# Moving the next head's queries and keys ahead of most value strips, and starting the output projection beside the last head, in a two-layer encoder trunk

## The chip, the cores and the metric

One core of one Trainium2 chip runs the whole kernel in one launch. The metric is the device time of one launch in microseconds, the median of a few runs. The engines are named as in the profile: PE is TensorE (matrix products), with PEld its weight loads; DVE is VectorE; ACT is ScalarE; POOL is GpSimd; SP is SyncE, which here only issues DMAs. Each engine runs its own instructions in a fixed order, and waits in that order.

## What is computed

The reference is a trunk of two layers over 1024 prompt tokens and 256 sample tokens, 1024 features wide, in float32. The change lies in layer 0, attention over a neighbourhood on a token grid 64 wide, with 16 heads of 64 features and a gate:

```
proj = h @ w_in ;  q, k, v, g = split(proj, 4)
for every row r of the grid, every head:
    s = q_r . k(rows around r, columns around) ;  s = where(mask, s + bias, -1e30)
    o = softmax(s) . v
return (o * silu(g)) @ w_out          # then + residual
```

Layer 1 is a gated delta network in chunks, which the change does not touch.

## The kernel before

**How numbers are held.** [...] A block of tokens is 512, 512 or 256 wide (`BLK`). `load_w` (L1085) brings a weight in: SP loads `wraw` (one buffer), `wh` is a cast of it on POOL while `a["hi"]` is set (L1094) and on ACT otherwise (L1096), and `wl` is a negative copy on ACT (L1100) to which a DMA issued by POOL adds the weight once more (L1101). `wh` and `wl` have three buffers each.

**The loop over heads** (L333). The attention of head h is a generator, and a small scheduler, `Side`, lets it advance by a step each time that the projection beside it has issued so many columns: `side.add(chain, delay, pace)` starts it `delay` columns from now, and each step's own distance is multiplied by `pace`. Beside head h's attention the loop issues the products of head h+1's queries and keys (`qk_head`, three blocks: 24 matmuls each of 512, 512 and 256 columns), and then, by h modulo 4: the gates of the next pair of heads (`g_pair`, h%4 of 1 and 2), or a part of the next four heads' values. These are ten strips of 128 tokens, V0 to V9, each 24 matmuls of 256 columns: strips 0 to 3 at h%4 of 3, strips 4 to 9 at the next h%4 of 0, ahead of `qk_head(h + 1)` (`v_quad`, L114). ACT and DVE each make one pass over a strip (L110, L111) to move it out of PSUM.

**One head.** `qk_head` ends with two DMAs on ACT's queue which copy the keys, in their high part KH (L195) and low part KL (L196), from the upper 64 partitions to the lower; the scores of the head need both. The attention has five units j of two score tiles: scores on PE (L279 with KH, L280 with KL; L298 and L299 for the sample tokens), softmax (DVE L216, ACT L217 with the exponential, DVE L218 and L219), transposes on PE into `pt` (L236), its split in `ph` on ACT (L240) and `pl` on DVE (L241), the products with the values into O (L256), and their way out with the gate (ACT L262, DVE L263 and L264). After an odd head the pair's O is spilled to DRAM (L323).

**After the loop** the spilled outputs of the first seven pairs are loaded back (L361) and split in OH (ACT, L362) and OL (L363: POOL for even k, DVE for odd k), and the output projection `w_o` runs, i = 0 to 7 by blocks b; its first evacuations are on DVE (L381). PSUM has three banks `mm` for projections.

**What sets the order.** The program's order gives each instruction its priority, and a list scheduler then orders each engine's queue from it when the kernel is built. So instructions that the text has after the loop can stand beside the last heads: the first output products do already in the kernel before.

```
            side.add(attention(h, qkk, V, G, O), 14000 if h % 4 == 1 else 2000, (1.6, 1.2, 1.5, 1.35)[h % 4])
            if h % 4 == 0:
                v_quad(q, V, [s for s in range(10) if s not in V], side)
            if h < 15:
                qkk = qk_head(h + 1, side)
```

Of the kernel before, what the change touches and what calls it, by code (L numbers as in the profile page):

```python
# [8 lines left out]
F32 = mybir.dt.float32  # L9
F32R = mybir.dt.float32r  # L10
BF16 = mybir.dt.bfloat16
AF = mybir.ActivationFunctionType
# [5 lines left out]
KD = 8  # L18
BLK = [(0, 512), (512, 512), (1024, 256)]
# [16 lines left out]
def layer0(ctx, tc, a, h1_out):  # L36
# [136 lines left out]
    with st:  # L173
# [92 lines left out]
        def attention(h, qkk, V, G, O):  # L266
# [55 lines left out]
            if h % 2 and h < 15:  # L322
                nc.sync.dma_start(a["o_dram"][h // 2], O)  # L323

        done = {}
        side = Side()
        a["hi"] = True
# [5 lines left out]
        for h in range(16):  # L333
            done[h] = 0
            G = GS[h // 2]
            V = nV if h % 4 == 0 else V
            side.add(attention(h, qkk, V, G, O), 14000 if h % 4 == 1 else 2000, (1.6, 1.2, 1.5, 1.35)[h % 4])
            side.tick(0)
            q = (h + 1) // 4
            if h % 4 == 0:  # L340
                v_quad(q, V, [s for s in range(10) if s not in V], side)
            if h < 15:
                qkk = qk_head(h + 1, side)
            if h % 4 in (1, 2) and h < 14:
                p = h // 2 + 1
                g_pair(p, GS[p], range(3), side)
            elif h % 4 == 3 and h < 15:
                nV = {}
                v_quad(q, nV, range(4), side)
            side.drain()  # L350
            if h % 2 and h < 15:
                O = ap.tile([128, T], F32, name="O", bufs=1)
        a["hi"] = False
        wo = [load_w(tc, a, a["w_o"][i]) for i in range(2)]
        OH, OL = parts(xp)
        for b, (t0, n) in enumerate(BLK):
            for k in range(KD):
                t = O[:, t0:t0 + n]
                if k < KD - 1:
                    t = OL[k][b].bitcast(F32)  # L360
                    nc.sync.dma_start(t, a["o_dram"][k, :, t0:t0 + n])  # L361
                nc.scalar.activation(OH[k][b], t, AF.Copy)  # L362
                (nc.vector if k % 2 else nc.gpsimd).tensor_sub(OL[k][b], t, OH[k][b])  # L363

    tc.keep_in_program_order(nc.scalar.preload_act_table_set("natural_log"))
    with pool(tc, "h1", 1) as hp, pool(tc, "rms1", 2) as rp, banks(tc, "pmm1", 2) as pmm1:
# [5 lines left out]
        for i in range(8):  # L372
            if i > 1:
                wo.append(load_w(tc, a, a["w_o"][i], raw=rp if i % 2 else None, keep=rp if i == 4 else None))
            h1 = hp.tile([128, NP], F32, name=f"p{i}")
            xt = rp.tile([128, NP], F32, name="xres")
            nc.sync.dma_start(xt, x_in[i, :, :NP])
            for b, (t0, n) in enumerate(BLK[:2]):
                ps = pmm.tile([128, 512], F32, name="mm")
                proj(nc, ps, *wo[i], OH, OL, b)  # L380
                nc.vector.tensor_add(h1.rearrange("p (r c) -> p c r", c=64)[:, 32 * b:32 * b + 32],  # L381
                                     nat(ps), nat(xt[:, t0:t0 + n]))
            nc.sync.dma_start(h1_out[i, :, :NP], h1)
            for b, (t0, n) in enumerate(BLK[:2]):
                H[b][i] = h1[:, t0:t0 + n]
                square(nc, rp, H[b][i], acc[b], i == 0)
# [751 lines left out]
                self.step(c)  # L1138


def proj_steps(nc, ps, wh, wl, XH, XL, b):
    for k in range(KD):
        for i, (w, x) in enumerate(((wh, XH), (wh, XL), (wl, XH))):
            nc.tensor.matmul(ps, w[:, k, :], x[k][b], start=(k == 0 and i == 0), stop=(k == KD - 1 and i == 2))  # L1144
            yield BLK[b][1]
# [20 lines left out]
def parts(xp):  # L1166

    return [[[xp.tile([128, n], F32R, name=f"x{p}{k}_{b}") for b, (t0, n) in enumerate(BLK)] for k in range(KD)]
            for p in "hl"]
# [228 lines left out]
```

## Time and profile before

| | |
|---|---|
| median of 3 runs | 2283.3 us (2281.1 to 2285.49) |
| the profiled execution | 2280.4 us, its span 2278.6 us |
| mean granted TensorE clock | 0.975 of full speed |
| busy: PE, DVE, ACT, POOL | 95%, 68%, 48%, 25% of the span |
| layer 0's heads in the span | about 85 to 685 us |

A row of the timeline gives the start from the span's beginning and the duration; matmuls overlap, so what one costs is the distance between the starts of two of them. The bracket behind a row is idle time of the engine before it, and what ended that.

### The profile page before, as it was taken

The page shows a single profiled execution, that of the slowest core. Times are in us where ns is not written, and L with a number is a line of the kernel's source. Part 1 is how long each engine was busy: PE and PEld are TensorE (multiplying, and loading weights), DVE is VectorE, ACT ScalarE, POOL GpSimd, SP SyncE. Part 2 cuts the span into 40 slices and gives each one's busy share as a digit, 9 for nine tenths or more (in the row PEclk, how much of TensorE's full clock was granted, in tenths as well). Part 3 has the DMA queues.
Part 4 walks back from the last instruction along what each step waited for, and adds up shares of the span by engine and source line. Part 5 has one row for each costly group of instructions (what it writes and reads, how often), then busy time and mean ns, then how long its engine had stood idle before and what let it go on. Part 6 is the DMA issues. An engine that isn't in the chain of part 4 may idle for free.

```text
span 2278.6 us, 34055 instructions
## 1 busy us (share of the span) xinstructions
PE 2171.5 (95%) x12502; PEld 1889.8 (83%) x12502; DVE 1545.8 (68%) x3419; ACT 1104.2 (48%) x2282; POOL 572.9 (25%) x621
## 2 busy tenths in 40 slices
PE   8999999899989889999899999999899999999998
PEld 7889889789768768888788888888788888877887
DVE  5676576576683649597687978878457666676444
ACT  6455445445462454434335445344356666654233
POOL 2110110111020332313223322233166766610000
PEclk9999999999999889999899999999899999999999
DMA  5443442434447244444354444553566656567322
GB/s 178 110 111 79 100 106 78 109 92 104 114 134 212 73 102 123 123 126 117 92 147 143 108 143 114 141 146 91 173 207 176 173 168 184 150 213 235 112 97 84
DMA packets 146119, 301.14 MB, mean 132 GB/s; under 512 B 44688, under 2 KB 67216, under 8 KB 144928
## 3 DMA queue, kind: packets, MB, share of 16 engines
q1 hardware_dynamic: 124480, 232.89, 32.6%
q0 software_dynamic: 12384, 45.09, 11.2%
q10 hardware_dynamic: 9088, 20.98, 3.1%
q8 instruction: 99, 1.62, 0.3%
q14 instruction: 68, 0.56, 0.1%
HBM read 212.97 MB, written 75.45 MB: 127 GB/s over the span
## 4 chain that ended last, share of the span: by engine, by line
PE 69%; DVE 15%; DMA 6%; ACT 5%; issue 3%; POOL 1%; SPq 0%; DVEq 0%; ACTq 0%; POOLq 0%
PE mm L1144 41%; PE mm L1160 4%; PE k L908 3%; DVE acc L460 3%; PE o L880 2%; PE u L880 2%; PE k L899 2%; PE o L921 2%; PE O L256 2%; DVE X L581 2%; DVE tmp L579 2%; PE pt L236 2%; DMA KH<-KH 1%; DMA vT<-qkv_spill 1%; PE m L607 1%
## 5 line engine op out<-in xcount | busy, mean ns | idle before, releaser
L1144 PE MATMUL mm<-xh,wh 128*128 128x512 f32 (+1 forms) x1920 | 701.8, 366 | 11.7 <-ACT wh L1096 5.9
L1144 PE MATMUL mm<-xh,wl 128*128 128x512 f32 (+1 forms) x1920 | 699.8, 365 | 4.7 <-DVE wl L1098 2.2
L1144 PE MATMUL mm<-xl,wh 128*128 128x512 f32 (+1 forms) x1920 | 702.2, 366 | 0.0
L1144 PEld LDWEIGHTS mm<-xh,wh 128*128 128x128 f32 x1920 | 369.2, 192 | 56.9 <-ACT wh L1096 6.4
L1144 PEld LDWEIGHTS mm<-xh,wl 128*128 128x128 f32 x1920 | 368.6, 192 | 47.5 <-DVE wl L1098 2.4
L1144 PEld LDWEIGHTS mm<-xl,wh 128*128 128x128 f32 x1920 | 369.1, 192 | 43.0 <-issue 0.2
L460 DVE SCALAR_TENSOR_TENSOR acc<-raw,cw,acc 128x1282 f32<-128x1282 f32 x128 | 203.1, 1587 | 43.1 <-ACT acc L458 41.5
L1096 ACT ACTIVATE wh<-wraw 128x1024 fp32r<-128x1024 f32 x94 | 98.9, 1055 | 110.9 <-PE mm L1144 88.0
L1094 POOL CAST wh<-wraw 128x1024 fp32r<-128x1024 f32 x30 | 31.5, 1049 | 473.6 <-PE mm L1144 339.7
L1144 PE MATMUL mm<-yh,wh 128*128 128x512 f32 (+1 forms) x384 | 137.5, 359 | 2.3 <-ACT yh L1018 1.9
L1144 PE MATMUL mm<-yh,wl 128*128 128x512 f32 (+1 forms) x384 | 137.0, 358 | 1.2 <-DVE wl L1098 1.2
L1144 PE MATMUL mm<-yl,wh 128*128 128x512 f32 (+1 forms) x384 | 137.7, 360 | 0.3 <-DVE yl L1019 0.3
L912 DVE TENSOR_TENSOR vl<-k,vh 128x256 fp32r<-128x256 f32 x160 | 67.1, 424 | 69.3 <-ACT vh L911 64.8
L463 ACT ACTIVATE th<-acc 128x1282 f32<-128x1282 f32 x32 | 40.9, 1277 | 149.4 <-DVE acc L460 149.4
L241 DVE TENSOR_TENSOR pl<-pt,ph 128x512 fp32r<-128x512 f32 (+2 forms) x144 | 75.4, 540 | 55.1 <-ACT ph L240 54.0
L240 ACT ACTIVATE ph<-pt 128x512 fp32r<-128x512 f32 (+2 forms) x144 | 67.3, 478 | 76.1 <-PE pt L236 69.1
L1100 ACT ACTIVATE wl<-wraw 128x1024 fp32r<-128x1024 f32 x86 | 90.8, 1055 | 22.4 <-PE mm L1144 9.4
L217 ACT ACTIVATE P<-P,mx 128x384 f32<-128x384 f32 (+1 forms) x128 | 74.9, 585 | 51.0 <-DVE mx L216 50.1
L455 ACT ACTIVATE raw<-mm 128x512 f32<-128x512 f32 (+1 forms) x96 | 49.4, 520 | 97.4 <-PE mm L1144 96.9
L1160 PE MATMUL mm<-wh,xl 128*128 128x256 f32 x320 | 92.3, 289 | 0.3 <-POOL xl L65 0.3
L1160 PE MATMUL mm<-wl,xh 128*128 128x256 f32 x320 | 92.1, 288 | 0.4 <-DVE wl L1098 0.4
L1160 PE MATMUL mm<-wh,xh 128*128 128x256 f32 x320 | 92.2, 289 | 0.0
(316 smaller groups left out, 4885.6 us busy)
## 6 DMA issues: line engine op xcount, KB each, us to landing
wraw<-w_qkv SPq DMA_DIRECT2D x32, 512.0 KB, 3.9
wl<-w_qkv POOLq DMA_DIRECT2D x32, 512.0 KB, 7.3
qkv_spill<-th SPq DMA_DIRECT2D x32, 512.0 KB, 2.7
wraw<-w_go SPq DMA_DIRECT2D x32, 512.0 KB, 3.6
Al<-e_spill SPq DMA_DIRECT2D x8, 1280.0 KB, 7.3
qe<-eg_spill SPq DMA_DIRECT2D x16, 640.0 KB, 8.1
wraw<-w_qk SPq DMA_DIRECT2D x16, 512.0 KB, 3.8
wl<-w_qk POOLq DMA_DIRECT2D x16, 512.0 KB, 9.0
```

Source lines behind the costliest of these rows:

```text
L217: nc.scalar.activation(Pv, Pv, AF.Exp, scale=-1.0, bias=mx[:, 0:1], accum_out=mx[:, 1:2])
L240: nc.scalar.activation(view(ph), view(pt), AF.Copy)
L241: nc.vector.tensor_sub(view(pl), view(pt), view(ph))
L455: nc.scalar.activation(r[:, t0 + o:t0 + o + n], ps[:, :n], AF.Copy)
L460: nc.vector.scalar_tensor_tensor(acc, r[:, i:i + m], cw[:, f, i:i + 1], acc, op0=OP.mult, op1=OP.add)
L880: self.tc.nc.tensor.matmul(ps, w[x], v[y], start=(first and i == 0), stop=(i == 2))
L908: nc.tensor.matmul(pw, W[:, d, cs[d]], Y[d], start=True, stop=True)
L912: nc.vector.tensor_sub(vl, pw, vh)
L1096: nc.scalar.activation(wh, raw, AF.Copy)
L1100: nc.scalar.activation(wl, raw, AF.Copy, scale=-1.0)
L1144: nc.tensor.matmul(ps, w[:, k, :], x[k][b], start=(k == 0 and i == 0), stop=(k == KD - 1 and i == 2))
L1160: nc.tensor.matmul(ps, x[k][b][:, cc], w[:, k % 4, :], start=(k == 0 and i == 0), stop=(k == KD - 1 and i == 2))
```

## The change

It does three things. At h%4 of 0 only strips 4 and 5 come before `qk_head(h + 1)`, and strips 6 to 9 behind it. The attention of the heads with h%4 of 1 starts 2000 columns after it is added instead of 14000, at pace 1.5 instead of 1.2, and heads 14 and 15 run at pace 0.75. And in the step of head 15 the first two `w_o` slices are loaded, the spilled outputs of blocks 0 and 1 are split (k = 0 to 6, the subtractions all on POOL), and three output products, (i, b) = (0,0), (1,0) and (0,1), are begun with k = 0 to 6, each holding one of the three `mm` banks; k = 7, which is head 14's and 15's own output, follows after the loop.

```diff
+        def o_parts(b, ks):
+            t0, n = BLK[b]
+            for k in ks:
+                t = O[:, t0:t0 + n]
+                if k < KD - 1:
+                    t = OL[k][b].bitcast(F32)
+                    nc.sync.dma_start(t, a["o_dram"][k, :, t0:t0 + n])
+                nc.scalar.activation(OH[k][b], t, AF.Copy)
+                (nc.vector if k % 2 and (b == 2 or k == KD - 1) else nc.gpsimd).tensor_sub(OL[k][b], t, OH[k][b])
...
-            side.add(attention(h, qkk, V, G, O), 14000 if h % 4 == 1 else 2000, (1.6, 1.2, 1.5, 1.35)[h % 4])
+            side.add(attention(h, qkk, V, G, O), 2000, 0.75 if h > 13 else (1.6, 1.5, 1.5, 1.35)[h % 4])
...
-                v_quad(q, V, [s for s in range(10) if s not in V], side)
+                v_quad(q, V, [s for s in (4, 5) if s not in V], side)
             if h < 15:
                 qkk = qk_head(h + 1, side)
+            else:
+                wo = [load_w(tc, a, a["w_o"][i]) for i in range(2)]
+                OH, OL = parts(xp)
+                for b in range(2):
+                    o_parts(b, range(KD - 1))
+                begun = {(i, b): pmm.tile([128, 512], F32, name="mm") for i, b in ((0, 0), (1, 0), (0, 1))}
+                for b in range(2):
+                    for k in range(KD - 1):
+                        for i in range(2 - b):
+                            for n in proj_steps(nc, begun[i, b], *wo[i], OH, OL, b, [k]):
+                                side.tick(n)
+            if h % 4 == 0:
+                v_quad(q, V, [s for s in range(10) if s not in V], side)
...
         a["hi"] = False
-        wo = [load_w(tc, a, a["w_o"][i]) for i in range(2)]
-        OH, OL = parts(xp)
-        for b, (t0, n) in enumerate(BLK):
-            for k in range(KD):
-                t = O[:, t0:t0 + n]
-                if k < KD - 1:
-                    t = OL[k][b].bitcast(F32)
-                    nc.sync.dma_start(t, a["o_dram"][k, :, t0:t0 + n])
-                nc.scalar.activation(OH[k][b], t, AF.Copy)
-                (nc.vector if k % 2 else nc.gpsimd).tensor_sub(OL[k][b], t, OH[k][b])
+        o_parts(0, [KD - 1])
+        o_parts(1, [KD - 1])
+        o_parts(2, range(KD))
...
-                proj(nc, ps, *wo[i], OH, OL, b)
+                ps = begun.get((i, b)) or pmm.tile([128, 512], F32, name="mm")
+                for n in proj_steps(nc, ps, *wo[i], OH, OL, b, [KD - 1] if (i, b) in begun else range(KD)):
+                    pass
```

The lines move down by 16 to 18, so the matmul of L1144 (queries, keys, gates, output) is L1162 in the changed kernel, that of L1160 (value strips) L1178, and L362 is L333.

**PE, from head 5's queries and keys to its first scores.** `mm_2996` is the first block of `qk_head(6)`, with the weights `wh_2988`; S_3034 before and S_3003 in the change are head 5's first scores, KH_2819 and KH_2601 its copied keys. Before, the scores come 28 products of `qk_head(6)` behind the end of `qk_head(5)`, and no value strip is left by then:

```order
L1144 MATMUL mm_2996<-xl7_0_136,wh_2988 128x512
L1144 MATMUL mm_2996<-xh7_0_112,wl_2989 128x512
L1144 MATMUL mm_3027<-xh0_1_92,wh_2988 128x512
L1144 MATMUL mm_3027<-xl0_1_116,wh_2988 128x512
L1144 MATMUL mm_3027<-xh0_1_92,wl_2989 128x512
L1144 MATMUL mm_3027<-xh1_1_95,wh_2988 128x512
L279 MATMUL S_3034<-KH_2819,Q_2818 128x256
L1144 MATMUL mm_3027<-xl1_1_119,wh_2988 128x512
L1144 MATMUL mm_3027<-xh1_1_95,wl_2989 128x512
L279 MATMUL S_3045<-KH_2819,Q_2818 128x384
```

In the change, where `mm_2933` is strip 9, their place is this:

```order
L1178 MATMUL mm_2933<-wh_2261,xh7_2_114 128x256
L1178 MATMUL mm_2933<-wl_2262,xh7_2_114 128x256
L1178 MATMUL mm_2933<-wh_2261,xl7_2_138 128x256
L256 MATMUL O_2977<-ph2_2957,V8_2930 128x256
L1162 MATMUL mm_2996<-xh0_0_91,wh_2988 128x512
L1162 MATMUL mm_2996<-xl0_0_115,wh_2988 128x512
L1162 MATMUL mm_2996<-xh0_0_91,wl_2989 128x512
L1162 MATMUL mm_2996<-xh1_0_94,wh_2988 128x512
L279 MATMUL S_3003<-KH_2601,Q_2600 128x256
L256 MATMUL O_2977<-ph2_2957,V9_2974 128x256
L256 MATMUL O_2977<-pl2_2958,V8_2930 128x256
L256 MATMUL O_2977<-pl2_2958,V9_2974 128x256
```

Strips 6 to 9, 96 matmuls with head 4's last units among them, now stand between the end of `qk_head(5)` and these rows; head 5's first scores come four products behind strip 9, and between strip 9 and the first product that uses it (V9_2974) are six matmuls.

**PE, beside head 1.** `KH_877` is head 1's copied keys, `mm_1204` and `mm_1235` the first two blocks of `qk_head(2)`. Before, head 1's first scores (S_1242) stand in the second block, behind the last products and transposes of head 0's sample tokens:

```order
L256 MATMUL O_1165<-pl2_1134,V6_616 128x256
L236 MATMUL pt_1176<-ident_60,Ps_1149 128x128 x3
L256 MATMUL O_1165<-pl1_1143,V5_613 128x128
L256 MATMUL O_1165<-pl2_1134,V7_644 128x256
L236 MATMUL pt_1176<-ident_60,Ps_1149 128x128
L1144 MATMUL mm_1235<-xh1_1_95,wh_1196 128x512
L279 MATMUL S_1242<-KH_877,Q_876 128x256
L280 MATMUL S_1242<-KL_878,Q_876 128x256
```

In the change they (S_1211, S_1223) stand in the first block, ahead of products (L256) and transposes (L236) of head 0:

```order
L1162 MATMUL mm_1204<-xh5_0_106,wh_1196 128x512
L1162 MATMUL mm_1204<-xl5_0_130,wh_1196 128x512
L1162 MATMUL mm_1204<-xh5_0_106,wl_1197 128x512
L279 MATMUL S_1211<-KH_877,Q_876 128x256
L279 MATMUL S_1223<-KH_877,Q_876 128x384
L1162 MATMUL mm_1204<-xh6_0_109,wh_1196 128x512
L256 MATMUL O_1119<-ph1_1095,V3_522 128x128
L256 MATMUL O_1119<-ph1_1095,V6_616 128x128
L256 MATMUL O_1119<-ph2_1086,V5_613 128x256
L256 MATMUL O_1119<-pl2_1087,V4_610 128x256
```

The row that comes in their new place before is the product with xh6_0_109, wh_1196, which moved down by two; the scores moved up by thirty rows of PE's order, and the first of them on KL by nineteen.

**ACT, in the last stage.** `xh_b_…<-xl_b_…` is OH of block b from a spilled output that a DMA brought; the two DMAs are head 15's keys. Before:

```order
L362 ACTIVATE xh_1_7572<-xl_1_7596 128x512
L362 ACTIVATE xh_2_7555<-xl_2_7579 128x256
L262 ACTIVATE t_7206<-O 64x256
L362 ACTIVATE xh_2_7558<-xl_2_7582 128x256
L362 ACTIVATE xh_2_7561<-xl_2_7585 128x256
L362 ACTIVATE xh_2_7564<-xl_2_7588 128x256
L190 ACTIVATE Q<-t 64x256
L191 ACTIVATE KH<-t 64x256
L240 ACTIVATE ph_7211<-pt 128x512
L195 DMA KH<-KH 64x1280
L196 DMA KL<-KL 64x1280
L240 ACTIVATE ph_7220<-pt 128x256
```

In the change:

```order
L240 ACTIVATE ph_7249<-pt 128x128
L333 ACTIVATE xh_2_7335<-xl_2_7359 128x256
L333 ACTIVATE xh_2_7338<-xl_2_7362 128x256
L333 ACTIVATE xh_2_7341<-xl_2_7365 128x256
L333 ACTIVATE xh_2_7344<-xl_2_7368 128x256
L1114 ACTIVATE wh<-wraw 128x1024
L217 ACTIVATE Ps,mx<-Ps,mx 128x256 x2
L190 ACTIVATE Q<-t 64x256
L191 ACTIVATE KH<-t 64x256
L262 ACTIVATE t_7297<-O 64x256
L195 DMA KH<-KH 64x1280
L196 DMA KL<-KL 64x1280
```

The copies of block 2 still stand ahead of the last query pass (`Q<-t 64x256`), with a weight's cast (`wh<-wraw`) beside them now; of head 14's own work, the exponentials of the sample tokens (`Ps`) moved ahead of the DMAs.

## Rows read from the trace of the kernel before

**Rows 1.** The page: the chain of work that ended last, its shares of the span by engine.

```profile
PE 69%; DVE 15%; DMA 6%; ACT 5%; issue 3%; POOL 1%; SPq 0%; DVEq 0%; ACTq 0%; POOLq 0%
```

**Rows 2.** Stretches of 20 us, all engines: the stretch, its length, then for PE, PEld (weight loads), DVE, ACT and POOL the busy us with the count of instructions, then the granted TensorE clock as a share of full speed, the DMA share and GB/s.

```profile
260.00:280.00 20.00, 17.09 (x94) 14.83 (x93) 11.74 (x31) 8.12 (x19) 1.91 (x2) 0.91 0.29 62
...
420.00:440.00 20.00, 15.67 (x88) 13.66 (x87) 11.54 (x31) 8.00 (x18) 1.87 (x2) 0.91 0.23 52
...
580.00:600.00 20.00, 16.71 (x99) 14.10 (x97) 13.85 (x39) 11.09 (x25) 0.86 (x1) 1.00 0.29 71
...
620.00:640.00 20.00, 13.57 (x61) 10.71 (x60) 13.46 (x27) 11.38 (x26) 8.84 (x7) 0.85 0.72 231
```

**Rows 3.** TensorE's timeline at heads 5, 9 and 13: start, duration, line, operation and tiles; in brackets the idle time before the instruction and what released it.

```profile
265.06 0.39 PE L279 MATMUL S<-KH,Q 128*128 128x256 f32 x1 [2.91 <-DMA KH<-KH]
...
269.19 0.40 PE L1144 MATMUL mm<-xh,wh 128*128 128x512 f32 x1
269.42 0.40 PE L1144 MATMUL mm<-xl,wh 128*128 128x512 f32 x1
...
282.84 0.55 PE L236 MATMUL pt<-ident,P 128*128 128x128 f32 x3 [0.77 <-DVE P L219]
...
425.27 0.39 PE L279 MATMUL S<-KH,Q 128*128 128x256 f32 x1 [4.33 <-DMA KH<-KH]
...
443.04 0.55 PE L236 MATMUL pt<-ident,P 128*128 128x128 f32 x3 [0.77 <-DVE P L219]
...
584.12 0.39 PE L279 MATMUL S<-KH,Q 128*128 128x256 f32 x1 [3.08 <-DMA KH<-KH]
```

**Rows 4.** GpSimd's timeline where head 5's projection ends and head 6's weights are loaded (same columns).

```profile
255.78 1.05 POOL L1094 CAST wh<-wraw 128x1024 fp32r<-128x1024 f32 x1 [11.88 <-PE mm L1144]
257.18 0.86 POOL L1101 DMA_DIRECT2D wl<-w_qk  x1 [0.35 <-ACT Q L190]
```

**Rows 5.** The line that adds the weights' low part by DMA (L1101), 150 to 660 us: from issue to landing.

```profile
DMA to landing us min/median/max: 6.5/8.4/10.8
```

**Rows 6.** Groups of instructions, 236 to 262 us, the two that move a value strip out of PSUM: busy us, mean ns of one, idle time before.

```profile
L111 DVE SCALAR_TENSOR_TENSOR V<-mm,rs,V 128x256 fp32r<-128x256 f32 x1 | 0.5, 484 | 0.0
L110 ACT ACTIVATE V<-mm,rs 128x256 fp32r<-128x256 f32 x1 | 0.5, 478 | 0.1
```

**Rows 7.** TensorE's timeline beside head 1, in the first block of `qk_head(2)`, and the wait of head 1's first scores.

```profile
101.10 0.39 PE L1144 MATMUL mm<-xh,wh 128*128 128x512 f32 x1
...
107.50 0.39 PE L280 MATMUL S<-KL,Q 128*128 128x256 f32 x1 [1.25 <-DMA KL<-KL]
```

**Rows 8.** ScalarE's timeline, the two copies of head 1's keys being issued on its queue.

```profile
96.62 0.47 ACTq L195 DMA_DIRECT2D KH<-KH  x1
97.53 0.47 ACTq L196 DMA_DIRECT2D KL<-KL  x1
```

**Rows 9.** The line of the first copy (L195), 90 to 110 us.

```profile
DMA to landing us min/median/max: 8.1/8.1/8.1
```

**Rows 10.** The line of the second copy (L196), 90 to 110 us.

```profile
DMA to landing us min/median/max: 9.9/9.9/9.9
```

**Rows 11.** TensorE's waits, 600 to 690 us: what it waited for, us in total, times, longest.

```profile
PE pt L236 <- DVE P L219: 5.1, 4, 2.7
PE pt L236 <- DVE mx L218: 3.3, 1, 3.3
```

**Rows 12.** TensorE's timeline in the last stage (between 643.17 and 644.00 stand six more matmuls of that width; 649.04 is the first of the output projection, 654.79 head 15's first scores).

```profile
643.17 0.28 PE L1144 MATMUL mm<-xh,wh 128*128 128x256 f32 x1
...
644.00 0.28 PE L1144 MATMUL mm<-xl,wh 128*128 128x256 f32 x1
...
649.04 0.63 PE L1144 MATMUL mm<-xh,wh 128*128 128x512 f32 x1
...
654.79 0.46 PE L279 MATMUL S<-KH,Q 128*128 128x256 f32 x2
...
684.44 0.51 PE L1144 MATMUL mm<-xh,wh 128*128 128x512 f32 x1 [1.38 <-DVE p L381]
```

**Rows 13.** ScalarE's waits, 600 to 690 us.

```profile
ACT xh L362 <- DMA xl<-o_spill: 5.0, 3, 2.5
```

**Rows 14.** VectorE's and then GpSimd's timeline, 633 to 637 us.

```profile
633.03 0.41 DVE L219 TENSOR_SCALAR P<-P,mx 128x384 f32<-128x384 f32 x1
...
633.43 1.72 DVE L363 TENSOR_TENSOR xl<-xl,xh 128x512 fp32r<-128x512 f32 x1
635.08 1.41 DVE L219 TENSOR_SCALAR P<-P,mx 128x384 f32<-128x384 f32 x1
...
633.34 2.94 POOL L363 TENSOR_TENSOR xl<-xl,xh 128x512 fp32r<-128x512 f32 x2 [2.27 <-ACT xh L362]
```

**Rows 15.** Groups of VectorE's instructions, 622 to 690 us: the low parts of the spilled outputs.

```profile
L363 DVE TENSOR_TENSOR xl<-xl,xh 128x512 fp32r<-128x512 f32 x6 | 6.7, 1112 | 1.9 <-ACT xh L362 1.9
```

**Rows 16.** One stretch from head 15's first softmax to the wait at 684.44 (columns as in rows 2).

```profile
656.30:684.50 28.20, 26.46 (x149) 20.50 (x147) 24.96 (x77) 20.71 (x52) 2.45 (x3) 1.00 0.34 94
```

**Rows 17.** Groups of VectorE's instructions in that stretch: count, busy us, mean ns of one, idle time before.

```profile
L263 DVE SCALAR_TENSOR_TENSOR t<-O,t 64x256 f32<-64x256 f32 x8 | 3.4, 421 | 0.7 <-ACT t L262 0.4
L264 DVE TENSOR_TENSOR O<-t,G 64x256 f32<-64x256 f32 x8 | 3.3, 417 | 0.2
...
L219 DVE TENSOR_SCALAR Ps<-Ps,mx 128x256 f32<-128x256 f32 x4 | 1.4, 349 | 0.0
```

More of the change, by code (lines that the diff above doesn't have):

```diff
@@ L378, in layer0 @@
             for b, (t0, n) in enumerate(BLK[:2]):
-                ps = pmm.tile([128, 512], F32, name="mm")
-                proj(nc, ps, *wo[i], OH, OL, b)
+                ps = begun.get((i, b)) or pmm.tile([128, 512], F32, name="mm")
+                for n in proj_steps(nc, ps, *wo[i], OH, OL, b, [KD - 1] if (i, b) in begun else range(KD)):
+                    pass
                 nc.vector.tensor_add(h1.rearrange("p (r c) -> p c r", c=64)[:, 32 * b:32 * b + 32],
@@ L1138, in drain, with proj_steps @@
                 self.step(c)
-def proj_steps(nc, ps, wh, wl, XH, XL, b):
-    for k in range(KD):
+def proj_steps(nc, ps, wh, wl, XH, XL, b, ks=range(KD)):
+    for k in ks:
         for i, (w, x) in enumerate(((wh, XH), (wh, XL), (wl, XH))):
```

## The prediction

> **What bounds the kernel now.** I read the chain of waits first: TensorE carries 69% of it [rows 1], so time is won only where TensorE stands idle or runs at its lower clock. Then the stretches of 20 us over the heads, to find where that is: the four weakest are those with heads 5, 9 and 13 in the step behind the value strips, and the last stage, 620 to 640, with 13.57 us busy at a clock of 0.85 [rows 2]. Then TensorE's timeline in each: in the first three the reader is to see one wait each of the same kind, the head's first scores on the DMA that copies its keys, 2.91, 4.33 and 3.08 us [rows 3]. In the last stage no DMA stands there but the softmax: the transposes wait 5.1 and 3.3 us for VectorE [rows 11]. Last I read what the new places lie beside: head 1's copies [rows 7 to 10], and the engines that feed the last stage [rows 13 to 17].
>
> The sum is made against the profiled execution, 2280.4 us, which is 2.9 us under the median of 2283.3; I carry the difference over to the median. About 0.2%, 4.6 us, is what a measurement of this kernel can tell from no change.
>
> **Heads 5, 9 and 13.** Between the end of a head's queries and keys and its first scores there now stand four value strips, 4 x 24 = 96 matmuls of 256 columns. Seven distances take 644.00 - 643.17 = 0.83 us [rows 12], 0.119 each, so 96 take 11.4 us, with head 4's (8's, 12's) last units on top, an estimate of 2.8 us more from the same distance for some 24 narrow products and transposes. That is 14.2 us, where head 1's copies, the only ones whose landing stands in the rows, took 8.1 and 9.9 us [rows 9, 10]. So the three waits go: 2.91 + 4.33 + 3.08 = 10.3 us.
>
> With them goes a clock loss. The granted clock was 0.91 in the two stretches with heads 5 and 9, and 1.00 at head 13, whose wait was as long [rows 2]: some of the matmuls behind the wait ran at the lower of the two levels. At 0.91 the busy time lost is 0.09 x 17.09 = 1.5 and 0.09 x 15.67 = 1.4, together 2.9 us. Two waits of 0.77 for a softmax come out of the crowding behind the late start [rows 3]; I count them as gone, 1.5 us. What is late next is strip 9: six matmuls behind its end TensorE wants it, and ScalarE and VectorE must move it out one after the other, 478 and 484 ns [rows 6]. The cover is one narrow and four wide products and one score, the wide ones 269.42 - 269.19 = 0.23 us apart [rows 3], so some 1.2 us against 0.96 and two hand-overs between engines. No row shows this wait; between nothing and 1.0 I take 0.5, three times, 1.5. Quads: -(10.3 + 2.9 + 1.5) + 1.5 = **-13.2 us**; bounds -16 (the new wait nothing, short remnants gone too) and -5 (the waits on the keys go, and head 4's crowded units wait some 3 us in each).
>
> The weights of the head after next are moved past too. Their cast is on GpSimd's queue and waits for a free buffer: before, 11.88 us for TensorE at 255.78; the adding DMA is issued 1.40 us later [rows 4] and lands within 6.5 to 10.8 [rows 5], so 12.2 us at worst. In the built program `wh_2988` takes the buffer of `qk_head(5)`, free when the strips begin, so the 14.2 us hide it: 0.
>
> **Head 1.** The shorter delay moves head 1's first scores up to where TensorE stood at 101.10 [rows 7]. Its key copies are issued as before, at 96.62 and 97.53 [rows 8], and landed 8.1 and 9.9 us later [rows 9, 10]: at 104.7 and 107.4. So a new wait of 3.6 us on KH; head 0's products, transposes and one wide product, about 1.8 us in all, stand between it and the first use of KL, which then waits another 0.9. The wait of 1.25 that stood there before [rows 7] goes. That is +3.3, and since two of three such waits were followed by a lower clock at 1.4 to 1.5 us, 1.0 more: **+4 us**, bounds +2 and +6.5. Behind the waiting scores on TensorE stand the last products of head 0, whose evacuations nobody needs at once.
>
> **The last stage.** Part of this is not new: in the kernel before the first output product already runs at 649.04, ahead of head 15's first scores at 654.79 [rows 12]. From 684.44, where the projection waits for a bank that VectorE frees, the order of TensorE is the same in both; so what counts is when that point comes. Three things bear on it.
>
> First, the start of head 15. Its keys are copied behind the copies of the spilled outputs on ScalarE, which waited 5.0 us for their loads [rows 13]. In the change fourteen of these and four of block 2 still stand ahead, and one cast of a weight with them. I take head 15's first softmax at the same 656.3: 0. If the 8.4 us of transpose waits [rows 11] and the clock loss, 0.15 x 13.57 = 2.0 [rows 2], went, it were -10.4; if the cast, the larger weight load ahead on SyncE's queue and two more exponentials came on top, +4.
>
> Second, VectorE behind it. It is busy 24.96 of 28.20 us from there [rows 16], 0.885, and sets the pace. Two of the eight pairs L263 and L264, 2 x (0.42 + 0.42), and two normalisations, 2 x 0.35 [rows 17], belong to head 14 and now come earlier: 2.4 us less, over 0.885, -2.7 us.
>
> Third, who subtracts. Six subtractions, 6.7 us, leave VectorE [rows 15], and six more come to GpSimd, 14 of them in all. Beside a pair of GpSimd's, 2.94 us, VectorE's normalisation took 1.41 us instead of 0.41 [rows 14]: 0.5 us lost for each, 3 us for six, so -3.7 for VectorE, in a stretch where it has room: 13.46 busy of 20 [rows 2]. 0. [...]
>
> Last stage: **-2.7 us**, bounds -13 and +4.
>
> **Sum.** -13.2 + 4 - 2.7 = -11.9; the profiled execution 2268.5, the median **2271**.
>
> **Rivals.**
> - *The last stage gives back its waits too.* If begun products keep TensorE busy beside head 14 and its transposes come in time, -10.4 more: 2261. For it: pace 0.75 brings head 14 forward. Against: the waits are the softmax's, which stands behind copies on ScalarE, and they stay there.
> - *The strips cover too little.* Head 4's units now stand beside products of 256 columns: twenty take 2.4 us where twenty wide ones took 4.6. If a unit's softmax needs all of the 4.6, it waits 2.2, two units in each of three quads: +13, and the sum is 1: 2284, no change. Against: both engines are half idle there, VectorE 11.74 us of 20 [rows 2].
> - *GpSimd blocks VectorE.* If each of the six added subtractions holds VectorE for its whole 2.94 / 2 = 1.47, that is 8.8 us, against the 6.7 that leave: +2.1 in place of -3.7, on the softmax's path +6: 2277. [...]
> - *Slower: the weights of heads 6, 10 and 14 come late.* If they had to take the value strips' buffer, free only at strip 9's end, 1.40 + 8.4 = 9.8 us [rows 4, 5] would be bare, three times 29 us: 2300. It decides from the point where cast and DMA take more than the strips' 14.2 us; in the profile after it would be a wait of the projection on the low part of a weight. Against: the buffer that it takes, and 12.2 at worst.
>
> **Chances.** The forecast 0.57, its own range 2265 to 2277; the last stage in full 0.14; the ports 0.08; the thin cover 0.15; late weights 0.06. Faster by over 0.2% (under 2278.7): 0.57 + 0.14 + 0.08 = 0.79; within 0.2%: 0.15; slower: 0.06. The range 2260 to 2284 leaves out the late weights, the lower half of the full last stage and the upper part of the thin cover, some 0.18.
>
> **What would show it.** Right: no wait of L279 on KH at heads 5, 9 and 13, stretches there at a clock of 1.00 and near 20 us busy; a wait on KH of some 3.6 us at about 101 us; the wait for the first evacuation, in its own time, some 12 us earlier than 684.44. Wrong: waits on the softmax between the strips, a strip's product waiting over 1 us, a weight's low part waited for, VectorE's normalisations over 1 us in the last stage. If the change as a whole moves less than 5 us, one of these has taken back what the keys gave.

## The result, and the profile after

The changed kernel took **2263.4 us** (median of 6 runs, 2260.5 to 2268.4) beside 2284.4 for the kernel before: ratio 0.991, 95% interval 0.9891 to 0.9929. Measured a second time, it took 2266.2 beside 2278.7: ratio 0.9937, interval 0.9916 to 0.9959. So it is faster, by 13 to 21 us; the forecast was 2271, 12 us. Its profiled execution has a span of 2259.6 us, at a mean clock of 0.976.

The stretches of 20 us, columns as in [rows 2], those that were weak before and the last stage:

```profile
260.00:280.00 20.00, 20.00 (x117) 17.31 (x116) 15.37 (x44) 12.41 (x28) 4.13 (x4) 1.00 0.45 91
420.00:440.00 20.00, 20.00 (x122) 17.53 (x121) 15.96 (x43) 10.94 (x27) 1.90 (x2) 1.00 0.49 117
580.00:600.00 20.00, 20.00 (x122) 17.44 (x122) 13.64 (x38) 9.51 (x23) 2.19 (x3) 1.00 0.52 122
600.00:620.00 20.00, 16.47 (x82) 12.74 (x81) 14.77 (x39) 13.43 (x31) 10.54 (x9) 0.95 0.81 256
620.00:640.00 20.00, 18.15 (x94) 15.33 (x94) 15.59 (x35) 14.24 (x33) 13.72 (x13) 0.88 0.42 109
```

The three with heads 5, 9 and 13 are now full, 20.00 us at a clock of 1.00. The weak stretch of the last stage has moved to 600 to 640, and GpSimd is busy there for 10.54 and 13.72 us, where [rows 2] had 8.84.

All of TensorE's waits from 85 to 600 us:

```profile
PE S L279 <- DMA KH<-KH: 3.5, 1, 3.5
PE pt L236 <- DVE mx L218: 0.7, 1, 0.7
PE S L280 <- DMA KL<-KL: 0.2, 1, 0.2
```

The waits on the keys' copies at heads 5, 9 and 13 [rows 3], and everything else behind 130 us, are gone. One new wait stands at head 1, as TensorE's timeline shows, which answers to [rows 7]:

```profile
104.57 0.56 PE L279 MATMUL S<-KH,Q 128*128 128x256 f32 x2 [3.50 <-DMA KH<-KH]
...
106.74 0.58 PE L280 MATMUL S<-KL,Q 128*128 128x256 f32 x1 [0.16 <-DMA KL<-KL]
...
108.08 0.63 PE L1162 MATMUL mm<-xl,wh 128*128 128x512 f32 x1
108.51 0.63 PE L1162 MATMUL mm<-xh,wl 128*128 128x512 f32 x1
```

It waits 3.50 us on KH, then 0.16 on KL, and the wide products behind it start 0.43 us apart, not 0.23: the lower clock (granted 0.66 from 104.5 to 109.5 us; from 95 to 115 it was 0.91, and 1.00 in the kernel before). In rows of the timeline `wh` and `wl` are the high and the low part of a weight, `xh` and `xl` those of the activations; the kernel makes each product over a slice of the features as three matmuls, (xh,wh), (xl,wh) and (xh,wl).

In the last stage, TensorE's waits from 600 to 690 us, beside [rows 11]:

```profile
PE mm L1162 <- DVE p L399: 3.4, 1, 3.4
PE pt L236 <- DVE mx L218: 1.9, 1, 1.9
PE pt L236 <- DVE P L219: 1.8, 2, 0.9
```

These waits for the softmax fell from 8.4 to 3.7 us, while four smaller ones beside them grew from 0.7 to 2.2 us in all, and the wait for the first evacuation grew from 1.38 [rows 12] to 3.44. It ends at 667.74 against 684.44: 16.7 us earlier, of which 16.2 were there already when head 14's keys were copied.

To see where time is won I take fixed points of the work: the issue of each head's key copy on ScalarE's queue (heads 1, 4, 7, 8, 11, 12, 14 and 15 here, from its timeline), and the first and the last evacuation of the output projection's first blocks.

```profile
96.43 0.47 ACTq L195 DMA_DIRECT2D KH<-KH  x1
...
202.92 0.47 ACTq L195 DMA_DIRECT2D KH<-KH  x1
...
316.99 0.47 ACTq L195 DMA_DIRECT2D KH<-KH  x1
...
354.49 0.47 ACTq L195 DMA_DIRECT2D KH<-KH  x1
...
468.60 0.47 ACTq L195 DMA_DIRECT2D KH<-KH  x1
...
506.10 0.47 ACTq L195 DMA_DIRECT2D KH<-KH  x1
...
582.68 0.47 ACTq L195 DMA_DIRECT2D KH<-KH  x1
...
634.96 0.47 ACTq L195 DMA_DIRECT2D KH<-KH  x1
```

The last evacuation, before and then changed, on VectorE's timeline:

```profile
755.50 1.09 DVE L381 TENSOR_TENSOR p<-mm,xres 128x512 f32<-128x512 f32 x1 [4.36 <-PE mm L1144]
```

```profile
741.08 1.09 DVE L399 TENSOR_TENSOR p<-mm,xres 128x512 f32<-128x512 f32 x1 [4.36 <-PE mm L1162]
```

The same points in the traces of all kernels give this table (us; the kernel before and the changed one were traced twice). Each point is the start of its instruction. The last column is what lies behind the last evacuation, where all of these kernels are the same.

| kernel | 1 to 4 | 4 to 7 | 8 to 11 | 12 to 14 | 14 to 15 | 14 to last evac. | 1 to last evac. | remainder |
|---|---|---|---|---|---|---|---|---|
| before | 102.4 | 121.6 | 122.7 | 80.5 | 50.1 | 156.7 | 658.9 | 1523.1 |
| e9_before_again | 102.2 | 121.4 | 121.7 | 80.9 | 50.2 | 156.7 | 658.0 | 1525.5 |
| changed | 106.5 | 114.1 | 114.1 | 76.6 | 52.3 | 158.4 | 644.7 | 1518.5 |
| e10_after_again | 107.7 | 114.1 | 114.3 | 76.4 | 53.5 | 160.9 | 648.4 | 1522.7 |
| e1_head1_late | 102.5 | 113.9 | 113.9 | 76.3 | 52.7 | 159.4 | 641.0 | 1515.6 |
| e2_quads_only | 101.9 | 114.2 | 114.1 | 76.5 | 50.7 | 156.9 | 638.7 | 1529.6 |
| e3_last_only | 102.2 | 122.0 | 122.6 | 81.9 | 55.4 | 161.5 | 665.2 | 1530.9 |
| e4_strips_only | 102.6 | 116.0 | 115.9 | 76.6 | 48.9 | 155.3 | 641.5 | 1519.4 |
| e5_longer_delay | 102.4 | 117.7 | 117.5 | 75.7 | 48.0 | 158.5 | 646.9 | 1522.8 |
| e6_half_on_dve | 101.6 | 114.1 | 114.1 | 76.6 | 50.6 | 156.9 | 638.3 | 1520.5 |
| e7_old_pace | 102.1 | 114.1 | 114.3 | 76.7 | 45.1 | 159.8 | 642.0 | 1521.3 |
| e8_quads_pace | 101.7 | 114.3 | 114.1 | 76.7 | 50.8 | 155.9 | 637.7 | 1515.2 |
| e11_all_on_dve | 101.8 | 114.2 | 114.3 | 76.5 | 48.4 | 154.6 | 636.5 | 1520.5 |
| e12_best | 102.5 | 114.1 | 114.3 | 76.5 | 50.0 | 154.0 | 636.4 | 1529.2 |

In the changed kernel head 1 costs 4.1 us, the strips win 7.5 + 8.6 + 3.9 = 20.0, and the last stage costs 1.7: 14.2 together. The other 4.8 us of that trace come before head 1's copy (0.2) and from the remainder (4.6).

### The profile page after: what moved, and what is told of

Its sections match the earlier page's. It is cut to its first block, busy times and chain, and to the rows that moved or that the text cites. A ratio compares the mean times of both kernels' runs of the same rounds, so it can differ in the third digit from the quotient of the medians.

```text
span 2259.6 us, 34076 instructions
## 1 busy us (share of the span) xinstructions
PE 2166.2 (96%) x12502; PEld 1885.5 (83%) x12502; DVE 1543.0 (68%) x3413; ACT 1103.8 (49%) x2280; POOL 582.1 (26%) x629
## 5 line engine op out<-in xcount | busy, mean ns | idle before, releaser
L1162 PE MATMUL mm<-xh,wh 128*128 128x512 f32 (+1 forms) x1920 | 701.2, 365 | 14.1 <-ACT wh L1114 5.9
L1162 PE MATMUL mm<-xh,wl 128*128 128x512 f32 (+1 forms) x1920 | 699.2, 364 | 5.2 <-DMA wl<-w_qkv 2.3
L1162 PE MATMUL mm<-xl,wh 128*128 128x512 f32 (+1 forms) x1920 | 701.6, 365 | 0.0
L1162 PEld LDWEIGHTS mm<-xh,wh 128*128 128x128 f32 x1920 | 368.5, 192 | 58.1 <-ACT wh L1114 6.4
L1162 PEld LDWEIGHTS mm<-xh,wl 128*128 128x128 f32 x1920 | 367.6, 191 | 48.0 <-DMA wl<-w_qkv 2.7
L1162 PEld LDWEIGHTS mm<-xl,wh 128*128 128x128 f32 x1920 | 368.1, 192 | 42.4 <-DVE xl L334 0.3
L1162 PE MATMUL mm<-yh,wh 128*128 128x512 f32 (+1 forms) x384 | 137.6, 360 | 1.9 <-ACT yh L1036 1.7
L1162 PE MATMUL mm<-yh,wl 128*128 128x512 f32 (+1 forms) x384 | 137.0, 358 | 1.2 <-DVE wl L1116 1.2
L1162 PE MATMUL mm<-yl,wh 128*128 128x512 f32 (+1 forms) x384 | 137.8, 360 | 0.3 <-DVE yl L1037 0.3
L241 DVE TENSOR_TENSOR pl<-pt,ph 128x512 fp32r<-128x512 f32 (+2 forms) x144 | 75.7, 539 | 49.1 <-ACT ph L240 48.2
L1178 PE MATMUL mm<-wh,xl 128*128 128x256 f32 x320 | 91.9, 287 | 0.6 <-POOL xl L65 0.6
L1178 PE MATMUL mm<-wl,xh 128*128 128x256 f32 x320 | 91.5, 286 | 0.6 <-DVE wl L1116 0.6
L929 ACT ACTIVATE vh<-k 128x256 fp32r<-128x256 f32 x160 | 60.5, 380 | 64.1 <-PE k L926 60.8
```

Of the source, the lines that this page charges most:

```text
L241: nc.vector.tensor_sub(view(pl), view(pt), view(ph))
L929: nc.scalar.activation(vh, pw, AF.Copy)
L1178: nc.tensor.matmul(ps, x[k][b][:, cc], w[:, k % 4, :], start=(k == 0 and i == 0), stop=(k == KD - 1 and i == 2))
```

## The experiments

Each ratio is to the kernel before, run beside it on the same chip, with its 95% interval.

**Head 1 back at its place.** From the changed kernel:

```diff
-side.add(attention(h, qkk, V, G, O), 2000, 0.75 if h > 13 else (1.6, 1.5, 1.5, 1.35)[h % 4])
+side.add(attention(h, qkk, V, G, O), 14000 if h == 1 else 2000,
+         1.2 if h == 1 else 0.75 if h > 13 else (1.6, 1.5, 1.5, 1.35)[h % 4])
```

> The changed kernel, with only head 1 put back to the delay of 14000 columns and the pace of 1.2 (heads 5, 9 and 13 keep 2000 and 1.5). Theory: head 1's new wait on its copied keys (3.5 us, then 0.2 on KL and 1.4 us at the lower clock) is a pure loss, so the second head's keys are copied at 122.5 us of the span again instead of 127.8, everything behind it moves forward by 3.9 us, and the time is 2259.5. Rival: the earlier start of head 1 is what puts heads 2 to 4 ahead and so frees the strips of heads 5, 9 and 13 from their softmax; then waits come back there and the time stays at 2263 or rises.

2261.2 us beside 2277.2, ratio 0.9929 (0.9902 to 0.9955). In the trace the wait on KH is gone, head 2's copy comes 25.9 us behind head 1's (31.3 in the changed kernel), and nothing came back at heads 5, 9 and 13. The early start is a pure loss of 4 us; the times alone could not have told it.

**Strips alone, and the last stage alone.** e2_quads_only is the kernel before with the split of the strips and the earlier start of heads 5, 9 and 13 (without head 1), e3_last_only with the third part of the change and the pace of 0.75 at heads 14 and 15:

```diff
 # e2_quads_only, from the kernel before
-side.add(attention(h, qkk, V, G, O), 14000 if h % 4 == 1 else 2000, (1.6, 1.2, 1.5, 1.35)[h % 4])
+side.add(attention(h, qkk, V, G, O), 14000 if h == 1 else 2000,
+         1.2 if h == 1 else (1.6, 1.5, 1.5, 1.35)[h % 4])
-                v_quad(q, V, [s for s in range(10) if s not in V], side)
+                v_quad(q, V, [s for s in (4, 5) if s not in V], side)
             if h < 15:
                 qkk = qk_head(h + 1, side)
+            if h % 4 == 0:
+                v_quad(q, V, [s for s in range(10) if s not in V], side)
```

> The kernel before, with only the value strips split round the next head's queries and keys and the delay of 2000 and pace of 1.5 at heads 5, 9 and 13 (head 1 and the last stage as before). Theory: the three steps give 7.5 + 8.6 + 3.9 = 20.0 us by the distances between the key copies in the two traces, so the time is some 2264, and the trace has no wait of TensorE between 130 and 600 us. Rival (the forecast's term): only 13.2 of it comes from here, and the rest from the last stage: 2271.

> The kernel before, with only the last stage changed (the parts of the output projection begun beside head 15, fourteen subtractions on GpSimd, pace 0.75 for heads 14 and 15). Theory: from the copy of head 14's keys to the shared point of the order it wins 0.6 us and then loses 2.2 at the lower clock behind a wait for the three banks (3.4 us instead of 1.4), so the time is 2285 to 2286, no change that can be measured. Rival (the forecast's term): -2.7, 2281.5; rival (the stage gives all its waits): 2271.

e2_quads_only: 2258.2 beside 2277.2, 0.9919 (0.9894 to 0.9944); 20.2 us won up to the last evacuation, and no wait of TensorE from 130 to 600 us. e3_last_only: 2289.3, 1.0057 (1.0035 to 1.0078). The theory of e2 holds, by its trace to 0.2 us. All three expectations of e3 missed: the last stage alone is slower. Of the 12 us between the medians, its trace shows 6.3 up to the last evacuation, 4.8 of them from head 14's copy on; the rest lies in a long remainder, 1530.9 us. So the strips carry the whole gain, and the new last stage takes some of it back.

**What in the strips does it.** e4_strips_only has the split of the strips from the diff above, but the delay of 14000 and the pace of 1.2 stay; e5_longer_delay leaves the strips and starts heads 5, 9 and 13 later:

```diff
 # e5_longer_delay, from the kernel before
-14000 if h % 4 == 1 else 2000
+14000 if h == 1 else 22000 if h % 4 == 1 else 2000
```

> The kernel before, with only the value strips split round the next head's queries and keys; the delay of 14000 columns and the pace of 1.2 stay for heads 1, 5, 9 and 13, so that the first scores come 28 products behind strip 9. Theory: the cover of the strips is what removes the waits on the keys, and the delay matters little: the three waits and the clock loss go, but the late start crowds head 5's units (9's, 13's) before the step ends, 1.0 to 1.6 us each as in the kernel before; 2267 to 2269. Rival: the shorter delay does the work and the strips alone give half at most: 2274 or more.

> The kernel before, with only the delay at heads 5, 9 and 13 raised from 14000 to 22000 columns; the value strips stay ahead of the queries and keys. The first scores of head 5 then come 43 products behind the end of its queries and keys, not 28: some 9.9 us by 0.23 us each, where the copies took 7.4 us and more. Theory: the waits on the copied keys (10.3 us in all) and the lower clock behind two of them (4.7 us by the distances) go, and the later start crowds the head's last units, some 1.5 us more in each of the three: from head 4's key copy to head 14's, 10 us less than before, while the split of the strips gave 17.4 to 20.2; time about 10 us under the kernel before. Rival: what the split gives is a matter of the whole order, the wait only moves to the end of the head: within 4 us of the kernel before.

e4_strips_only: 2259.5 beside 2277.2, 0.9929 (0.9904 to 0.9955). TensorE's waits from 130 to 600 us, where each of the three heads has a short one on the softmax left:

```profile
PE pt L236 <- DVE P L219: 2.1, 3, 0.8
PE O L256 <- DVE pl L241: 0.5, 2, 0.3
PE S L298 <- DVE mx L216: 0.2, 1, 0.2
```

e5_longer_delay: 2267.1 beside 2281.2, 0.9939 (0.9921 to 0.9958). Its waits, same stretch:

```profile
PE S L298 <- DVE mx L216: 3.1, 3, 1.1
PE S L280 <- DMA KL<-KL: 2.9, 3, 1.2
```

Both won more than expected. From head 1's copy to head 14's, e4 wins 16.1 us, e5 13.9, the strips with the shorter delay 20.5. What counts is that the copies land behind other work, whichever; the later start wins two thirds of it and still waits on KL (2.9 us) and on the sample tokens' scores (3.1), which the strips take away too.

**What in the last stage costs.** Three kernels move its parts one by one, all with head 1 late. Subtractions, where "big" are those of 512 columns, six of them odd:

```diff
 # e6_half_on_dve, from e1_head1_late: 8 big ones on POOL, 6 on DVE
-(nc.vector if k % 2 and (b == 2 or k == KD - 1) else nc.gpsimd)
+(nc.vector if k % 2 else nc.gpsimd)
 # e11_all_on_dve, from e1_head1_late: none on POOL, 14 on DVE
-(nc.vector if k % 2 and (b == 2 or k == KD - 1) else nc.gpsimd)
+(nc.vector if k % 2 or b < 2 else nc.gpsimd)
```

> The changed kernel with head 1's late start (as e1_head1_late), and the subtractions of the spilled outputs for odd k back on VectorE, eight of the large ones left on GpSimd. Theory: VectorE takes 6 x 1.1 = 6.7 us back and loses less to GpSimd beside it (in the changed kernel its normalisation took 633 ns on the mean instead of 420, and two passes of the queries 1344 instead of 686, 4 us in all): head 15's keys are copied 2 to 3 us later than in e1_head1_late, counted from head 14's copy (52.7 us there). [...]

> The changed kernel with head 1's late start (as e1_head1_late) and the fourteen subtractions of blocks 0 and 1 all on VectorE, none of these on GpSimd. With all on GpSimd head 15's keys were copied 52.7 us behind head 14's, with six on VectorE 50.6. Theory (GpSimd beside VectorE costs each pass that meets it): the rest of VectorE's passes fall back to their usual lengths (the normalisation near 420 ns), and the eight further subtractions, 8 x 0.68 = 5.4 us, cost VectorE less than the 15 us of GpSimd did: 49 to 51. Rival: VectorE is full there, and the subtractions come on top: 53 or more.

e6: 2254.7 beside 2281.2, 0.989 (0.987 to 0.9909). e11: 2257.1 beside 2278.7, 0.9908 (0.9885 to 0.993). From head 14's copy to head 15's: 52.7 us with fourteen big subtractions on GpSimd, 50.6 with eight, 48.4 with none; to the last evacuation 159.4, 156.9, 154.6. The first of these orders came out at 52.3, 52.7 and 53.5 us in three traces (changed, e1, e10), so the step of 4.3 is clear of that scatter. VectorE's groups from 575 to 665 us (count, busy us, mean ns of one), first with fourteen (e1_head1_late), then with eight (e6), then with none (e11):

```profile
L219 DVE TENSOR_SCALAR P<-P,mx 128x384 f32<-128x384 f32 x15 | 8.3, 562 | 0.4
...
L192 DVE TENSOR_TENSOR Q<-t,Q 64x512 fp32r<-64x512 f32 x3 | 3.3, 1094 | 0.2
```

```profile
L219 DVE TENSOR_SCALAR P<-P,mx 128x384 f32<-128x384 f32 x15 | 7.7, 516 | 0.2
...
L192 DVE TENSOR_TENSOR Q<-t,Q 64x512 fp32r<-64x512 f32 x2 | 1.4, 684 | 0.1
```

```profile
L219 DVE TENSOR_SCALAR P<-P,mx 128x384 f32<-128x384 f32 x15 | 6.2, 417 | 0.2
...
L192 DVE TENSOR_TENSOR Q<-t,Q 64x512 fp32r<-64x512 f32 x2 | 1.4, 684 | 0.1
```

The normalisation falls from 562 to 516 to 417 ns. The theory of e6 was wrong: head 15's keys were copied 2.1 us earlier than in e1_head1_late, not 2 to 3 later. A subtraction on GpSimd, 1.36 us on the mean in e1 and 1.70 in e6, costs this stretch more than the same one on VectorE, where it takes 0.68 us. Between the two key copies VectorE was busy 38.84, 38.01 and 36.21 us, although the last figure has eight of the subtractions in it. One thing stays open: the list scheduler ordered TensorE's queue of this stage differently in the three, so the longer passes are shown, but how much of the 4.8 us is theirs alone is not.

The pace, taken out of the changed last stage (e7, from e1_head1_late) and put alone on e2 (e8):

```diff
 # e7_old_pace, from e1_head1_late
-1.2 if h == 1 else 0.75 if h > 13 else (1.6, 1.5, 1.5, 1.35)[h % 4]
+1.2 if h == 1 else (1.6, 1.5, 1.5, 1.35)[h % 4]
 # e8_quads_pace, from e2_quads_only
-1.2 if h == 1 else (1.6, 1.5, 1.5, 1.35)[h % 4]
+1.2 if h == 1 else 0.75 if h > 13 else (1.6, 1.5, 1.5, 1.35)[h % 4]
```

> The changed kernel with head 1's late start (as e1_head1_late), with the paces of heads 14 and 15 back at 1.5 and 1.35. Theory: the last stage is as long as head 15's chain of softmax and products on VectorE, and the pace only shifts matmuls that fill it: the distance from head 14's key copy to the first evacuation of the output projection stays within 1.5 us of e1_head1_late's 85.6. Rival: the dense pace starves TensorE at the end (its wait of 3.4 us for the banks, and the lower clock behind it), and without it that wait is 1.4 and 2 to 4 us are won.

> The strips split and the shorter delay at heads 5, 9 and 13 (as e2_quads_only), the last stage as before but for the pace of 0.75 at heads 14 and 15. From head 14's key copy to the last evacuation of the output projection e2_quads_only took 157.0 us, and the three runs with the whole new last stage 158.4 to 161.5. Theory: the new stage loses by the banks that it holds and the lower clock behind, not by the pace: 157, the time that of e2_quads_only. Rival: the pace is what costs: 159 to 161.

e7: 2263.0 beside 2281.2, 0.9925 (0.9909 to 0.9941); 85.2 us from head 14's copy to the first evacuation against 85.6, although head 15's keys come 7.6 us earlier. What the earlier start wins is spent again behind it; that VectorE's work for head 15 sets the end, as the theory has it, is not shown by this. e8: 2252.3, 0.9888 (0.9866 to 0.991), 155.9 us to the last evacuation against 156.9; e12_best below, with the same order in this stage, took 154.0. So the pace alone wins 1 to 3 us in the old last stage and nothing in the new one. To the first evacuation e8 and e12 need 81.0 and 80.2 us, e11 80.9: no run shows a gain from beginning the output projection early. The old stage with this pace and all subtractions on VectorE was not run.

**Controls, and a better version.** The two kernels of this case once more, and e8 with head 1 at 16000 columns instead of 14000.

> The kernel before, unchanged, as a control. Theory: what lies behind the last evacuation of the output projection (1515 to 1531 us in the traces of kernels that are the same there) varies from one execution to the next by where the lower clock falls, not by the kernel; so a second trace of this kernel has the same 658.9 us from head 1's key copy to that evacuation within 1 us, and a remainder that differs from 1523.1 by several us; the verdict is a ratio of 1.000 within 0.002. Rival: the remainder belongs to the kernel, by the moment at which it starts: again 1523 within 1.

> The changed kernel once more, as it is. Theory: from head 1's key copy to the last evacuation 644.7 us again within 1, the remainder another one than 1518.5; the ratio to the kernel before is nearer to what the first part alone gives (14.2 of 2280, 0.994) than the first measurement's 0.991. Rival: 0.991 again, and the remainder is shorter in the changed kernel for a reason of its own.

> The strips split, the shorter delay at heads 5, 9 and 13, pace 0.75 at heads 14 and 15, the last stage otherwise as before (as e8_quads_pace), and head 1 at 16000 columns in place of 14000, so that its first scores stand behind the landing of both key copies. Theory: no wait on KL at head 1 (0.6 to 1.4 us in the others), from head 1's key copy to the last evacuation 637 us, 7 to 8 less than the changed kernel; the time 7 us below e10_after_again. Rival: the last stage's new form wins something that its trace hides: within 2 us of e10_after_again.

The kernel before against itself: 0.9994 (0.998 to 1.0008), and from head 1's copy to the last evacuation 658.0 us against 658.9; its remainder was 1525.5, 2.4 us longer. The changed kernel: 0.9937, nearer to its first part, which itself came out 3.7 us longer than the first time, with 1.2 of it at head 1 and 2.5 in the last stage: "within 1" was too narrow. The remainder was 1522.7, not 1518.5. e12_best: 2257.0 beside 2278.7, 0.99 (0.9877 to 0.9924), 9.2 us under the changed kernel beside it, and 12.0 in the part up to the last evacuation (636.4 against 648.4). It beats the kernel before clearly, and the changed one by trace and median, though the intervals of the two ratios overlap a little. Its own step, head 1 at 16000 columns, won nothing: the wait on KL went as expected, but TensorE then waits 1.4 us for softmaxes (three waits from 85 to 600 us), and head 1 to head 4 takes 102.5 us, against 102.4 in the kernel before.

## Why the prediction was right, and where its terms were not

The sum, -12, met a measured -13 to -21, and -10 to -14 in the part that the change touches. That it came so near is partly luck: two of its terms were off in opposite ways, one by 7 us and one by more than 4.

1. **Head 1, +4 us: right.** 4.1 and 5.5 in two traces, with the wait of 3.50 us where 3.6 was forecast; the wait on KL was 0.16, not 0.9, and the rest goes with the lower clock (0.91 from 95 to 115 us). e1_head1_late takes it away whole.
2. **Heads 5, 9 and 13, -13.2 us: the mechanism right, the term too small by 7.** It measured -20.0. The waits on the keys went as forecast (10.3), and the two on the softmax (1.5). The rest was mis-sized. Idle time and slow time come apart in the stretches between the copies, first before, then in the changed kernel (columns as in [rows 2]):

```profile
199.07:320.63 121.56, 116.44 (x759) 104.90 (x758) 79.35 (x220) 58.96 (x140) 11.64 (x13) 0.99 0.40 98
358.12:480.83 122.71, 116.44 (x759) 104.89 (x758) 79.33 (x220) 58.98 (x140) 11.65 (x13) 0.99 0.40 97
518.32:598.83 80.51, 76.63 (x534) 70.80 (x534) 50.30 (x142) 39.39 (x93) 7.17 (x8) 1.00 0.40 96
```

```profile
202.92:316.99 114.07, 114.07 (x759) 103.88 (x758) 78.79 (x220) 59.60 (x140) 12.03 (x13) 1.00 0.43 104
354.49:468.60 114.11, 114.06 (x759) 103.83 (x758) 78.77 (x220) 59.61 (x140) 11.95 (x13) 1.00 0.42 104
506.10:582.68 76.58, 76.47 (x537) 70.95 (x536) 51.73 (x146) 40.25 (x95) 8.09 (x9) 1.00 0.42 101
```

Idle fell by 5.1, 6.2 and 3.8 us, 15.1 in all: besides the waits of the sum, 2.9 us on the sample tokens' scores, for which the sum had no term. Before, 85 to 600 us:

```profile
PE S L298 <- DVE mx L216: 2.9, 3, 1.2
```

The busy time fell by 2.4, 2.4 and 0.2, 4.9 in all for the same matmuls but three, where 0.09 of TensorE's busy time gave 2.9. And the wait that I charged for strip 9, 1.5, never came: no wait of TensorE is left there. 2.9 + 2.0 + 1.5 and two remnants of 0.25 are the missing 7. The weights came in time, as forecast.
3. **The last stage, -2.7 us: wrong.** It cost 1.7 and 4.2 us in the two traces. The sum was made for the end of the wait for a bank (684.44 before). Counted from head 14's copy, that came 0.6 us earlier in one trace of the changed kernel and 2.1 later in the other, and the rest of the loss lies behind it (point 4). The second reason was right in direction: from head 15's first softmax on it took 26.5 us in both traces instead of 27.8, half of the 2.7. The first was put at 0, but that softmax came 0.7 and 3.5 us later behind head 14's copy than before, and head 15's keys were copied 52.3 and 53.5 us behind head 14's, against 50.1. That is the stretch of the third reason, and its step is the one that failed, "in a stretch where it has room". VectorE had room on the average, but the passes that GpSimd met are those on the softmax's path. In the changed kernel, VectorE and then GpSimd:

```profile
617.73 1.24 DVE L219 TENSOR_SCALAR P<-P,mx 128x384 f32<-128x384 f32 x1
...
625.24 1.47 DVE L219 TENSOR_SCALAR P<-P,mx 128x384 f32<-128x384 f32 x1
...
628.02 1.72 DVE L192 TENSOR_TENSOR Q<-t,Q 64x512 fp32r<-64x512 f32 x1
...
613.65 15.54 POOL L334 TENSOR_TENSOR xl<-xl,xh 128x512 fp32r<-128x512 f32 x12 [1.83 <-ACT xh L333]
```

Twelve subtractions run without a pause for 15.54 us, and beside them the normalisation takes 1.24 and 1.47 us instead of 0.42, a pass of the queries 1.72 instead of 0.68: the sign of being wrong that the prediction named, normalisations over 1 us. This is the rival that I gave 0.08, with a price of +6: with the fourteen subtractions on VectorE (e11_all_on_dve) the way to the last evacuation is 4.8 us shorter. These passes are up to 1.05 us longer beside subtractions of 1.3 us each (15.54 for twelve); why they are, no run shows.
4. **The end of the stage.** The same wait for a bank, 1.38 us before, is 3.44 us in the changed kernel, where the three products begun early hold all three banks. Behind it the clock fell to the lower level; the stretches, changed kernel first:

```profile
667.00:672.00 5.00, 4.26 (x10) 3.42 (x11) 2.42 (x3) 4.99 (x7) 0.86 (x1) 0.50 0.52 156
```

```profile
684.00:689.00 5.00, 4.56 (x20) 3.79 (x21) 2.27 (x3) 4.99 (x7) 0.86 (x1) 1.00 0.57 165
```

0.50 against 1.00: the way from the first evacuation to the last takes 74.5 us instead of 72.1. My sum had no term for it. It is not due to the begun products alone. That stretch in e2_quads_only and in e8_quads_pace, both with the old last stage, behind waits for the bank of 2.3 and 2.5 us:

```profile
662.66:734.80 72.14, 71.06 (x314) 58.87 (x315) 23.60 (x28) 18.37 (x25) 4.31 (x5) 1.00 0.59 177
```

```profile
659.19:734.14 74.95, 73.87 (x314) 60.91 (x315) 23.67 (x27) 18.37 (x25) 4.33 (x5) 0.95 0.59 170
```

In all traces it took 72.1 us at a clock of 1.00 (before, e9, e2, e4) or 73.7 to 75.0 at 0.95 to 0.98 (the ten others, e5, e8 and e12 without begun products among them).
5. **Behind the stage: "the order is the same".** True, but not worth zero in one measurement: the remainder was between 1515.2 and 1530.9 us in fourteen traces, with the same number of instructions on every engine. The shortest (e8_quads_pace) and the longest (e3_last_only):

```profile
734.14:2249.30 1515.16, 1443.33 (x8152) 1250.33 (x8150) 1062.61 (x2158) 726.79 (x1435) 486.68 (x532) 0.97 0.49 141
```

```profile
761.17:2292.11 1530.94, 1458.46 (x8152) 1263.76 (x8150) 1060.99 (x2158) 725.47 (x1435) 484.48 (x532) 0.96 0.47 139
```

Of the 15.8 us between them 15.1 are TensorE's busy time, for the same 8152 matmuls at another clock. One place shows how: TensorE waits 2.1 us for the same instruction in the kernel before and in the changed one,

```profile
PE m L607 <- ACT X L594: 2.1, 1, 2.1
```

```profile
PE m L625 <- ACT X L612: 2.1, 1, 2.1
```

and the 5 us behind it, before and then changed:

```profile
935.00:940.00 5.00, 5.00 (x21) 4.61 (x21) 0.20 (x1) 2.54 (x5) 0.00 (x0) 0.50 0.08 26
```

```profile
919.50:924.50 5.00, 5.00 (x37) 4.56 (x36) 0.19 (x1) 3.59 (x6) 0.00 (x0) 1.00 0.08 26
```

0.50 and 21 matmuls against 1.00 and 37. What decides it stays open. The two ratios of the changed kernel, 0.991 and 0.9937, lie within each other's reach (their intervals overlap), and most of the difference comes from the kernel before, whose median was 2284.4 us the first time and 2278.7 the second.

## What to carry to other kernels

The waits on the copies at heads 5, 9 and 13, 10.3 us, went when work was put behind the copies' issue, and 20.0 us were won: look for work that nobody needs yet, and check which waits behind the first one go with it, the clock's loss included. When a helper engine gets more work beside an engine that has room on the average, look at the passes that stand on the critical chain: in the kernel before VectorE was busy for 13.46 of 20 us of the last stage [rows 2], and with more of GpSimd's work passes on that chain became up to 1.05 us longer. Where one part of a change moves several microseconds and the rest of the kernel scatters by fifteen, compare fixed points of the trace, not medians.

## What the runs showed of the hardware

- In the changed kernel VectorE's tensor_scalar pass of 128x384 took 0.42 us on the mean from 130 to 570 us, where GpSimd makes no subtraction of the spilled outputs, and up to 1.47 beside one; its pass of the queries of 64x512 took 0.68 there, 1.72 beside one. GpSimd's large subtraction took 1316 ns on the mean in the changed kernel and 1359 in e1_head1_late, where all fourteen are its own; where VectorE makes six of them it took 1695 in e6_half_on_dve and 1350 in the kernel before.
- A wait of about the same length was followed by the lower clock in some places and not in others: 3.08 us at head 13 was not (granted 1.00 from 584 to 588 us), 2.91 and 4.33 were (0.50 from 266 to 268 and from 426 to 429) [rows 2, 3]; the wait for the bank was not at 2.3 us in e2_quads_only (clock 1.00 from 662 to 667 us) and was at 2.1 us in e5_longer_delay (0.69 from 669 to 674); and the 2.1 us of point 5 only in one of two traces.
